# Long convolutions in one float32 pass, with the pointwise stage in place in PSUM and a skewed order on VectorE and ScalarE

## The chip, the cores and the metric

The kernel runs on one core of a Trainium2 chip. The metric is the device time of one execution in microseconds (us); 3 runs of the kernel before gave 2292.52, 2295.47 and 2297.69, so its median is 2295.47 us. All engines are named as the profile names them: PE is TensorE, PEld its weight loads, DVE VectorE, ACT ScalarE, POOL GpSimd, SP SyncE (here it only issues DMAs).

## The reference, cut to what matters

The model is a two-layer diffusion backbone of 512 latent and 256 context tokens with 1024 channels. Layer 0 mixes tokens with an order-2 Hyena long convolution, and then has a mixture of experts; layer 1 has attention and another mixture of experts. The change touches only the long convolutions of layer 0:

```python
def long_conv(z, K):
    L = z.shape[1]
    Z = jnp.fft.rfft(z.astype(jnp.float32), n=2 * L, axis=1)
    y = jnp.fft.irfft(Z * K[None], n=2 * L, axis=1)[:, :L]
    return y.astype(z.dtype)

def hyena_mix(h, w_in, b_in, conv_w, conv_b, ..., skip, w_out, b_out):
    u = short_conv(h @ w_in + b_in, conv_w, conv_b)
    v, x1, x2 = jnp.split(u, 3, axis=-1)
    K = hyena_filter_spectrum(L, ...)
    z = v
    for o, gate in enumerate((x1, x2)):
        z = gate * (long_conv(z, K[:, o]) + skip[o] * z)
    return z @ w_out + b_out
```

It runs once on the latent tokens (part x, 512 long) and once on the context tokens (part c, 256 long). The adaLN rows (`silu(c) @ ada_w + ada_b`) are a large product that has nothing to do with the convolution, and part of it is done beside it.

## The kernel before, in words

The transform is a product with tables of cosines and sines, split into even and odd frequencies. `hyena_conv` works through 8 units: 2 orders times 4 groups of 256 channels. A unit has three parts: x0, x1 (two halves of the latent frequencies) and c. In one unit's stretch of the program PE does, in this order: the forward products of part x0 (F0, tile ps_f), a turn of four 128x128 transposes that brings a third of the next unit's input into tile ps_z (T0), then F1, T1, F2, T2; then four products of the adaLN rows (`next(fill)`, L248), the inverse products of the unit before for its first 128 channels (I0, tile ps_y), adaLN products again, and I1. The first unit has no inverse beside it, and after the eighth there is a ninth stretch with inverses only. F0 to F2 here are names for PE's work; in the code F is the table of the transform.

Accuracy comes from splitting: a float32 value is held as a rounded high part and a low part (`split`, an ACT cast, L202, and a DVE subtraction, L203), and each product is three matmuls on fp32r operands (high by high, high by low, low by high; L726 forward, L769 inverse). The tables came in split form from the stage that computes the filter spectra (`k.F`), so they are in SBUF when the convolution starts. The context's inverse (L764) is already a plain float32 product.

Between forward and inverse product lies the pointwise stage of a part: ACT copies one half of ps_f to SBUF (L730), DVE forms sum and difference (L732, L733) into tile fab, the complex product with the spectrum kt is done by POOL (L737, L740) and DVE (L738, L739), DVE forms sum and difference once more (L741, L742), and the result is split into yh and yl (L748, L749). Each finished inverse is gated by DVE into U (L773). The spectra kt and the gates gx come from DRAM by SP's DMAs (L694, L699), each spectrum 512 KB, and the inputs hx were written there by POOL's DMAs (L665) in the stage before.

The order of PE is as the code is written (`tc.manual_schedule` for PE alone); those of DVE, ACT, POOL and SP are chosen by a scheduler, by its own estimates. On every engine the instructions run in the order that is fixed at build time, and one that waits holds up all behind it. PSUM has three buffers under tag a (ps_f, ps_y), one under tag b (ps_z) and one under tag m (ps_ada and ps_adaT): `Psum(k, a=3, b=1, m=1)`. The turn of the next unit (L709) thus needs ps_z to be read out by what reads it.

## Time and profile before

| what | value |
|---|---|
| median of 3 runs | 2295.47 us |
| profiled execution | 2298.74 us (3.27 above the median) |
| span in its trace, first to last instruction | 2296.9 us |
| mean granted TensorE clock over the span | 0.957 of full speed |
| PE, DVE, ACT, POOL busy | 89%, 56%, 33%, 21% of the span |
| convolution stage, first F0 to last inverse product | 376.3 to 590.1 us |

The shares are averages over stages with different limits. The convolution is 213.8 us, 9.3% of the span; what happens in it has to be read from windows of the trace over this stretch, and the end of it is followed by the output projection, which needs the last inverse. The eight F0 start at 376.3, 391.6, 422.7, 450.3, 474.7, 502.6, 525.7 and 551.6 us.

### The profile page before, as it was taken

The page shows a single profiled execution, that of the slowest core. Times are in us where ns is not written, and L with a number is a line of the kernel's source. Part 1 is how long each engine was busy: PE and PEld are TensorE (multiplying, and loading weights), DVE is VectorE, ACT ScalarE, POOL GpSimd, SP SyncE. Part 2 cuts the span into 40 slices and gives each one's busy share as a digit, 9 for nine tenths or more (in the row PEclk, how much of TensorE's full clock was granted, in tenths as well). Part 3 has the DMA queues.
Part 4 walks back from the last instruction along what each step waited for, and adds up shares of the span by engine and source line. Part 5 has one row for each costly group of instructions (what it writes and reads, how often), then busy time and mean ns, then how long its engine had stood idle before and what let it go on. Part 6 is the DMA issues. An engine that isn't in the chain of part 4 may idle for free.

```text
span 2296.9 us, 33948 instructions
## 1 busy us (share of the span) xinstructions
PE 2035.5 (89%) x13738; PEld 1196.9 (52%) x13738; DVE 1276.9 (56%) x2230; ACT 751.2 (33%) x1470; POOL 482.7 (21%) x472
## 2 busy tenths in 40 slices
PE   5899998788895999999999979999987698888797
PEld 2788887667672333333333269899756232222232
DVE  5877676999544344434344587787766133223233
ACT  4544443221332333222332245555533121111111
POOL 3333324666242000000000064243213000000000
PEclk9999999889896999999999979999998799999998
DMA  7434336545646999897997531111384999999996
GB/s 277 159 111 143 126 111 231 192 152 187 226 162 247 385 392 361 326 385 300 388 374 308 205 117 39 55 38 38 120 308 185 343 409 409 409 409 409 409 409 258
DMA packets 174342, 580.72 MB, mean 253 GB/s; under 512 B 11934, under 2 KB 42786, under 8 KB 167914
## 3 DMA queue, kind: packets, MB, share of 16 engines
q1 hardware_dynamic: 165226, 545.96, 62.4%
q0 software_dynamic: 8960, 32.59, 4.0%
q8 instruction: 108, 1.77, 0.3%
q14 instruction: 48, 0.39, 0.1%
HBM read 546.97 MB, written 31.54 MB: 252 GB/s over the span
## 4 chain that ended last, share of the span: by engine, by line
PE 49%; DMA 15%; DVE 12%; issue 3%; ACT 2%; POOL 1%; SPq 0%; DVEq 0%; POOLq 0%; ACTq 0%
PE ps_U L1225 10%; PE ps_Y L1225 9%; PE ps_G L1225 8%; PE ps_qkv L1653 6%; DMA raw<-in_moe_up_dram 5%; DMA raw<-in_moe_gate_dram 5%; PE ps_o L846 4%; DMA raw<-in_moe_down_dram 3%; PE ps_s L1401 3%; PE ps_sc L1721 1%; PE ps_pv L1752 1%; PE ps_H L1191 1%; DVE p L738 1%; DVE p L742 1%; DVE p L739 1%
## 5 line engine op out<-in xcount | busy, mean ns | idle before, releaser
L1225 PE MATMUL ps_Y<-raw,a 128*32 128x512 f32 (+1 forms) x1536 | 295.3, 600 | 28.5 <-DMA raw<-in_moe_down_dram 24.1
L1225 PE MATMUL ps_U<-raw,H 128*32 128x512 f32 (+1 forms) x1536 | 298.1, 597 | 17.0 <-DMA raw<-in_moe_up_dram 16.8
L1225 PE MATMUL ps_G<-raw,H 128*32 128x512 f32 (+1 forms) x1536 | 300.5, 606 | 12.8 <-DMA raw<-in_moe_gate_dram 11.7
L1225 PEld LDWEIGHTS ps_Y<-raw,a 128*32 128x32 f32 (+1 forms) x1536 | 78.4, 119 | 219.9 <-issue 171.3
L1180 POOL DMA_INDIRECT xe<-hscr,idxi x24 | 22.3, 927 | 728.4 <-PE ps_H L1191 655.2
L1225 PEld LDWEIGHTS ps_U<-raw,H 128*32 128x32 f32 (+1 forms) x1536 | 75.0, 118 | 186.2 <-issue 146.2
L1225 PEld LDWEIGHTS ps_G<-raw,H 128*32 128x32 f32 (+1 forms) x1536 | 76.6, 120 | 175.5 <-issue 153.1
L1653 PE MATMUL ps_qkv<-qwh,hh 128*128 128x256 f32 x512 | 154.0, 301 | 0.1
L1653 PE MATMUL ps_qkv<-qwl,hh 128*128 128x256 f32 x512 | 146.2, 285 | 3.8 <-POOL qwl L203 2.3
L1653 PE MATMUL ps_qkv<-qwh,hl 128*128 128x256 f32 x512 | 145.7, 285 | 0.0
L1268 DVE TENSOR_TENSOR up<-ps_U,lr 64x512 f32<-64x512 f32 (+1 forms) x48 | 41.2, 859 | 187.7 <-ACT lr L1265 182.6
L1268 DVE TENSOR_TENSOR sg<-ps_G,lr 64x512 f32<-64x512 f32 (+1 forms) x48 | 41.3, 859 | 162.9 <-ACT lr L1265 162.7
L1265 ACT COPY lr<-ps_Y 64x512 f32<-64x512 f32 (+1 forms) x47 | 33.8, 719 | 281.7 <-PE ps_Yc L1225 143.9
L1268 DVE TENSOR_TENSOR up<-ps_Y,lr 64x512 f32<-64x512 f32 (+1 forms) x47 | 40.0, 852 | 152.3 <-ACT lr L1265 152.3
L1225 PE MATMUL ps_Gc<-raw,H 128*32 128x512 f32 x512 | 121.4, 595 | 0.0
L1225 PE MATMUL ps_Uc<-raw,H 128*32 128x512 f32 x512 | 119.7, 596 | 0.0
L1225 PE MATMUL ps_Yc<-raw,a 128*32 128x512 f32 x512 | 116.6, 593 | 0.0
L1653 PEld LDWEIGHTS ps_qkv<-qwh,hh 128*128 128x128 f32 x512 | 98.9, 193 | 6.7 <-issue 4.9
L1653 PEld LDWEIGHTS ps_qkv<-qwl,hh 128*128 128x128 f32 x512 | 99.1, 194 | 4.6 <-POOL qwl L203 2.7
L642 PE MATMUL ps_u<-hh,wl 128*128 128x512 f32 (+1 forms) x384 | 101.3, 340 | 0.0
L642 PE MATMUL ps_u<-hh,wh 128*128 128x512 f32 (+1 forms) x384 | 100.9, 339 | 0.0
L642 PE MATMUL ps_u<-hl,wh 128*128 128x512 f32 (+1 forms) x384 | 100.7, 339 | 0.0
(475 smaller groups left out, 4786.9 us busy)
## 6 DMA issues: line engine op xcount, KB each, us to landing
raw<-in_moe_gate_dram SPq DMA_DIRECT2D x128, 1024.0 KB, 9.7
raw<-in_moe_up_dram SPq DMA_DIRECT2D x128, 1024.0 KB, 10.6
raw<-in_moe_down_dram SPq DMA_DIRECT2D x128, 1024.0 KB, 10.5
raw<-in_ada_w_dram SPq DMA_DIRECT2D x48, 1024.0 KB, 5.2
raw<-in_w_in_dram SPq DMA_DIRECT2D x12, 1024.0 KB, 5.4
raw<-in_w_qkv_dram SPq DMA_DIRECT2D x12, 1024.0 KB, 5.1
hx<-u POOLq DMA_DIRECT2D x24, 384.0 KB, 2.8
gx<-hx SPq DMA_DIRECT2D x16, 384.0 KB, 3.1
```

Of the source, the lines that this page charges most:

```text
L642: nc.tensor.matmul(ps[:, o:o + n], ww[:, d], ha[:, d, o:o + n], start=d == 0 and i == 0, stop=d == DC - 1 and i == 2)
L738: nc.vector.tensor_tensor(p1, ab, kv[:, :, 0:1].to_broadcast(shp), op=ALU.mult)
L739: nc.vector.tensor_tensor(p1[:, :, 0], p1[:, :, 0], p2[:, :, 1], op=ALU.subtract)
L742: nc.vector.tensor_tensor(p2[:, 1], p1[:, 0], p1[:, 1], op=ALU.subtract)
L846: nc.tensor.matmul(ps, a[d][:, tk], b, start=d == 0 and j == 0, stop=d == DC - 1 and j == 2 and bias is None)
L1191: nc.tensor.transpose(pt[:, d, :r], src[:r, c * P:(c + 1) * P], k.ident[:r, :r])
L1225: nc.tensor.matmul(ps[p0:p0 + n], st, w, start=start, stop=stop, tile_position=(0, p0))
L1265: nc.scalar.copy(t[:64], ps[64:])
L1268: nc.vector.tensor_tensor(out[:64, cs], ps[:64], t[:64], op=ALU.add)
L1401: nc.tensor.matmul(ps, o[:, c * P:(c + 1) * P], y[:, nb * 512:nb * 512 + 512], start=n == 0, stop=n == 2 * len(srcs) - 1)
L1653: nc.tensor.matmul(ps, a[:, d, tk], b, start=d == 0 and i == 0, stop=d == DC - 1 and i == 2)
L1721: nc.tensor.matmul(pss[m][:, o:o + n], a[r, tk], b[r, o:o + n], start=i == 0, stop=i == 2)
```

## The change

Nothing ahead of the convolution and nothing behind it changes its order on any engine. Within it:

- Forward and inverse products are one plain float32 matmul each in place of three fp32r matmuls; z and y are no longer split. The trace writes a plain float32 matmul as two records (L1775 and L764 of before are such).
- The tables Fx0, Fx1 (512 KB each), Fc0, Fc1 and idftx are loaded anew in float32 by SP's DMAs, in the pool of the convolution; the split ones stay where they are, unused. The SBUF range of Fx0 overlaps that of one of the input stage's tiles u, which is the source of the last write of hx (the DMA at L665), so its load waits for that write.
- The pointwise stage works in place in ps_f: sum and difference by DVE back into PSUM, one ACT copy of the whole tile (1024 columns) into fab, the second product by POOL from fab, the first by DVE in PSUM, the combination by DVE in PSUM, one ACT copy and a last DVE sum and difference into y. POOL has one instruction per part where it had three.
- From the first unit to the eighth the order of DVE and ACT is fixed as the code is written. Each part is cut into `begin`, `combine` and `end`, and the last two of a part stand inside the `begin` of the next part.

```diff
-    F, IE = k.F, {}
-    TILES = {"zh": ([P, 6, Q], F32R, 2, ca), "zl": ([P, 6, Q], F32R, 2, ca), "kt": ([P, 4, Q], F32, 4, ca),
-             "fab": ([P, 2, 2, Q], F32, 2, ca), "p1": ([P, 2, 2, Q], F32, 2, ca), "p2": ([P, 2, 2, Q], F32, 2, ca),
-             "yh": ([P, 2, 2, Q], F32R, 4, cb), "yl": ([P, 2, 2, Q], F32R, 4, cb), "p2c": ([P, 2, 2, Q], F32, 2, cb)}
+    F, IE = {}, {}
+    TILES = {"z": ([P, 6, Q], F32, 2, ca), "kt": ([P, 4, Q], F32, 4, ca),
+             "e": ([P, 2, Q], F32, 3, ca), "fab": ([P, 2, 2, Q], F32, 3, ca), "p2": ([P, 2, 2, Q], F32, 3, ca),
+             "y": ([P, 2, 2, Q], F32, 4, cb), "yc": ([P, 2, 2, Q], F32, 2, cb)}
...
-            Z[q, o] = tile_of("zh"), tile_of("zl")
-        zh, zl = Z[q, o]
+            Z[q, o] = tile_of("z")
...
-        pv = pt.rearrange("p c j t -> p c (j t)")
-        split(k, zh[:, 2 * c2:2 * c2 + 2], zl[:, 2 * c2:2 * c2 + 2], pv)
+        nc.scalar.copy(Z[q, o][:, 2 * c2:2 * c2 + 2], pt.rearrange("p c j t -> p c (j t)"))
...
-        for par, (Fh, Fl) in enumerate(F[pt]):
+        for par in range(2):
             for s in range(2):
-                n = 0
                 for h in range(nh):
...
-                    for w, m in ((fh, a), (fh, b), (fl, a)):
-                        nc.tensor.matmul(pk[:, par, s], w, m, start=n == 0, stop=n == 3 * nh - 1)
-                        n += 1
-        p2 = tile_of("p2" if pt == "x" else "p2c")
+                    nc.tensor.matmul(pk[:, par, s], F[pt][par][:, h, s, fs], z[:, c0 + par * nh + h],
+                                     start=h == 0, stop=h == nh - 1)
+        y = Y[q, o, pt, j] = tile_of("y" if pt == "x" else "yc")
+        return pk, y, kt.rearrange("p (a s) q -> p a s q", a=2), [tile_of(n) for n in ("e", "fab", "p2")]
+
+    def begin(f, prev):
+        pk, y, kv, (e, ab, p2) = f
+        shp = [P, 2, 2, Q]
         nc.scalar.copy(e, pk[:, 0])
...
+        if prev:
+            combine(prev)
+        nc.vector.tensor_tensor(pk[:, 0], e, pk[:, 1], op=ALU.add)
+        nc.vector.tensor_tensor(pk[:, 1], e, pk[:, 1], op=ALU.subtract)
+        nc.scalar.copy(ab, pk)
+        if prev:
+            end(prev)
         nc.gpsimd.tensor_tensor(p2, ab, kv[:, :, 1:2].to_broadcast(shp), op=ALU.mult)
-        nc.vector.tensor_tensor(p1, ab, kv[:, :, 0:1].to_broadcast(shp), op=ALU.mult)
-        nc.vector.tensor_tensor(p1[:, :, 0], p1[:, :, 0], p2[:, :, 1], op=ALU.subtract)
...
+        nc.vector.tensor_tensor(pk, pk, kv[:, :, 0:1].to_broadcast(shp), op=ALU.mult)
+
+    def combine(f):
+        pk, y, kv, (e, ab, p2) = f
+        nc.vector.tensor_tensor(pk[:, :, 0], pk[:, :, 0], p2[:, :, 1], op=ALU.subtract)
+        nc.vector.tensor_tensor(pk[:, :, 1], pk[:, :, 1], p2[:, :, 0], op=ALU.add)
+        nc.scalar.copy(e, pk[:, 0])
+
+    def end(f):
+        pk, y, kv, (e, ab, p2) = f
+        nc.vector.tensor_tensor(y[:, 0], e, pk[:, 1], op=ALU.add)
+        nc.vector.tensor_tensor(y[:, 1], e, pk[:, 1], op=ALU.subtract)
...
-                        for w, m in ((a, ih), (a, il), (b, ih)):
-                            nc.tensor.matmul(out, w, m, start=n == 0, stop=n == 6 * nf - 1)
...
+                for n in range(2 * nf):
+                    f, s = n // 2, n % 2
+                    t = IE[pt][:, par, f, s] if pt == "c" else F["x"][1][:, f, s] if par else IE["x"][:, f, s]
+                    nc.tensor.matmul(out, Y[q, o, pt, f][:, par, s, js], t, start=n == 0, stop=n == 2 * nf - 1)
...
+    for pt, L, nf in (("x", LX, 2), ("c", LC, 1)):
+        n = nf * L
+        F[pt] = [cb.tile([P, nf, 2, L // 2], F32, name="F%s%d" % (pt, par)) for par in range(2)]
+        for par, t in enumerate(F[pt]):
+            nc.sync.dma_start(t.rearrange("p a b c -> p (a b c)"), k.A["dft" + pt][:, par * n:par * n + n])
     load(*units[0])
     load(*units[1])
-    IE["x"], = load_dft(k, [cb], "idftx", (2, 2, LX // 2))
+    IE["x"] = cb.tile([P, 2, 2, LX // 2], F32, name="idftx")
+    nc.sync.dma_start(IE["x"].rearrange("p a b c -> p (a b c)"), k.A["idftx"])
...
+    order = tc.manual_schedule(engines=ORDERED)
+    order.__enter__()
     for i in range(len(units) + 1):
...
+        f = None
         if i < len(units):
             load_gates(*units[i])
+        else:
+            order.__exit__(None, None, None)
         for c2 in range(3):
             if i < len(units):
-                forward(*units[i], *parts[c2])
+                g = forward(*units[i], *parts[c2])
+                begin(g, f)
+                f = g
...
@@ -802,6 +810,9 @@
             next(fill, None)
             if i:
                 inverse(*units[i - 1], j)
+            if f and j == 0:
+                combine(f)
+                end(f)
```

Three places show how the instructions stand. First ACT's row for one unit in the middle, before; p2 is the copy of ps_f, zh the cast of a turn, yh the cast of the result:

```order
L730 COPY p2_4273<-ps_f_4248 128x512
L202 CAST zh_4291<-ps_z_4293 128x512
L730 COPY p2_4325<-ps_f_4300 128x512
L202 CAST zh_4291<-ps_z_4343 128x512
L730 COPY p2c_4363<-ps_f_4350 128x512
L202 CAST zh_4291<-ps_z_4375 128x512
L748 CAST yh_4285<-p2_4273 128x512 x2
L748 CAST yh_4337<-p2_4325 128x512 x2
```

The casts of the turns stand directly behind the copies of the forward products. Now the same for the change, where e is the copy of ps_f (L730, and L746 a second one after the combination), fab the copy of the whole tile and z that of a turn:

```order
L730 COPY e_4134<-ps_f_4124 128x512
L735 COPY fab_4135<-ps_f_4124 128x1024
L709 COPY z_4143<-ps_z_4144 128x512
L730 COPY e_4160<-ps_f_4150 128x512
L746 COPY e_4134<-ps_f_4124 128x512
L735 COPY fab_4161<-ps_f_4150 128x1024
L709 COPY z_4143<-ps_z_4174 128x512
L730 COPY e_4186<-ps_f_4180 128x512
L746 COPY e_4160<-ps_f_4150 128x512
```

The copy of turn T1, the second z here, stands behind the second fab, which reads what DVE's sum and difference of part x1 wrote.

On DVE, the change's row around those: L733 and L734 are sum and difference, L739 the product, L743 and L744 the combination with POOL's product p2, L750 and L751 the end:

```order
L733 TENSOR_TENSOR ps_f_4124<-e_4134,ps_f_4124 128x512
L734 TENSOR_TENSOR ps_f_4124<-e_4134,ps_f_4124 128x512
L739 TENSOR_TENSOR ps_f_4124<-ps_f_4124,kt_3975 128x1024
L743 TENSOR_TENSOR ps_f_4124<-ps_f_4124,p2_4136 128x2x256
L744 TENSOR_TENSOR ps_f_4124<-ps_f_4124,p2_4136 128x2x256
L733 TENSOR_TENSOR ps_f_4150<-e_4160,ps_f_4150 128x512
L734 TENSOR_TENSOR ps_f_4150<-e_4160,ps_f_4150 128x512
L750 TENSOR_TENSOR y_4133<-e_4134,ps_f_4124 128x512
L751 TENSOR_TENSOR y_4133<-e_4134,ps_f_4124 128x512
L739 TENSOR_TENSOR ps_f_4150<-ps_f_4150,kt_3977 128x1024
```

The sum and difference of the second part (tile ps_f_4150) stand behind the combination of the first (ps_f_4124), and this reads p2, which POOL computes from the first fab.

The second place is SP's queue at the start of the stage, from the third input on, before:

```order
L690 DMA U2_3801<-hx2_795 128x768
L694 DMA kt_3820<-kscr_00x0_401 128x1024
L694 DMA kt_3822<-kscr_00x1_436 128x1024
L694 DMA kt_3824<-kscr_00c0_523 128x1024
L690 DMA U3_3802<-hx3_796 128x768
L694 DMA kt_3828<-kscr_01x0_1121 128x1024
L781 DMA iec_3840<-in_idftc_dram 128x256
L782 DMA iec_3840<-in_dftc_dram 128x256
L699 DMA gx_3866<-hx8_801 128x768
L699 DMA gx_3866<-hx9_802 128x768
```

and now:

```order
L690 DMA U2_3801<-hx2_795 128x768
L775 DMA Fx0_3818<-in_dftx_dram 128x1024
L775 DMA Fx1_3819<-in_dftx_dram 128x1024
L775 DMA Fc0_3822<-in_dftc_dram 128x256
L775 DMA Fc1_3823<-in_dftc_dram 128x256
L694 DMA kt_3828<-kscr_00x0_401 128x1024
L694 DMA kt_3830<-kscr_00x1_436 128x1024
L694 DMA kt_3832<-kscr_00c0_523 128x1024
L690 DMA U3_3802<-hx3_796 128x768
L694 DMA kt_3836<-kscr_01x0_1121 128x1024
L779 DMA idftx_3842<-in_idftx_dram 128x1024
L782 DMA iec_3844<-in_idftc_dram 128x256
L783 DMA iec_3844<-in_dftc_dram 128x256
L699 DMA gx_3868<-hx8_801 128x768
```

The four tables F (L775) have moved ahead of all spectra kt, and idftx ahead of iec.

The third place is the end of the first group of adaLN rows, on DVE: L251 adds the bias to what PE summed in ps_ada, and PE's transposes of its result (L261) come right behind turn T2 in the stretch of the fifth unit. Before:

```order
L741 TENSOR_TENSOR p2_4542<-p1_4547 128x512
L742 TENSOR_TENSOR p2_4542<-p1_4547 128x512
L251 TENSOR_TENSOR adarow_4003<-ps_ada_4005,adarow_4003 128x512
L739 TENSOR_TENSOR p1_4585<-p1_4585,p2c_4580 128x2x256
L749 TENSOR_TENSOR yl_4555<-p2_4542,yh_4554 128x512
L773 SCALAR_TENSOR_TENSOR U5_3804<-ps_y_4642,invx_221,gx_4245 128x512
L773 SCALAR_TENSOR_TENSOR U5_3804<-ps_y_4642,invc_222,gx_4245 128x256
L741 TENSOR_TENSOR p2c_4580<-p1_4585 128x512
L742 TENSOR_TENSOR p2c_4580<-p1_4585 128x512
L732 TENSOR_TENSOR fab_4709<-p2_4707,ps_f_4682 128x512
L733 TENSOR_TENSOR fab_4709<-p2_4707,ps_f_4682 128x512
```

and now:

```order
L733 TENSOR_TENSOR ps_f_4456<-e_4462,ps_f_4456 128x512
L734 TENSOR_TENSOR ps_f_4456<-e_4462,ps_f_4456 128x512
L750 TENSOR_TENSOR y_4435<-e_4436,ps_f_4426 128x512
L751 TENSOR_TENSOR y_4435<-e_4436,ps_f_4426 128x512
L739 TENSOR_TENSOR ps_f_4456<-ps_f_4456,kt_4257 128x1024
L251 TENSOR_TENSOR adarow_3953<-ps_ada_3955,adarow_3953 128x512
L266 COPY modT_625<-ps_adaT_4488 128x4x2 x4
L768 SCALAR_TENSOR_TENSOR U6_3805<-ps_y_4497,invx_221,gx_4259 128x512
L768 SCALAR_TENSOR_TENSOR U6_3805<-ps_y_4497,invc_222,gx_4259 128x256
```

The addition stood ahead of the sums and differences of the unit whose turns precede the transposes (L732 and L733 of a new ps_f); now it stands behind the product of that unit's third part.

## Rows read from the trace of the kernel before

**Rows 1.** Busy time in stretches; columns stand in the first line.
```profile
core 0: us, PE busy (x) PEld busy (x) DVE busy (x) ACT busy (x) POOL busy (x), PEclk, DMA share, GB/s
422.70:450.30 27.60, 22.34 (x156) 18.89 (x154) 27.60 (x29) 5.78 (x10) 15.85 (x10) 0.81 0.47 169
...
551.64:590.10 38.46, 29.85 (x220) 26.19 (x219) 35.55 (x46) 14.85 (x24) 27.51 (x17) 0.87 0.40 138
376.30:590.10 213.80, 169.29 (x1213) 145.21 (x1214) 208.37 (x235) 55.36 (x94) 136.25 (x78) 0.88 0.54 191
```

**Rows 2.** DVE's costliest groups, 370 to 600 us: busy us, mean ns | idle before.
```profile
L738 DVE TENSOR_TENSOR p<-fab,kt 128x1024 f32<-128x1024 f32 x24 | 48.1, 2004 | 0.0
...
L773 DVE SCALAR_TENSOR_TENSOR U<-ps_y,invx,gx 128x512 f32<-128x512 f32 x16 | 11.9, 741 | 1.8 <-PE ps_y L764 1.8
...
L732 DVE TENSOR_TENSOR fab<-p,ps_f 128x512 f32<-128x512 f32 x16 | 10.8, 676 | 2.5 <-ACT p L730 2.5
...
L742 DVE TENSOR_TENSOR p2c<-p 128x512 f32<-128x512 f32 x8 | 5.4, 678 | 0.0
```

**Rows 3.** Timeline of DVE: start us, us, instruction.
```profile
431.38 0.68 DVE L732 TENSOR_TENSOR fab<-p,ps_f 128x512 f32<-128x512 f32 x1
431.97 0.68 DVE L733 TENSOR_TENSOR fab<-p,ps_f 128x512 f32<-128x512 f32 x1
```

**Rows 4.** Waits, 376 to 590 us: total us, times, longest.
```profile
PE ps_z L709 <- DVE zl L203: 31.7, 13, 4.3
```

**Rows 5.** Timeline of PE at the start: start us, us, instruction.
```profile
376.32 0.38 PE L726 MATMUL ps_f<-zh,dftx0h 128*128 128x256 f32 x1 [0.34 <-ACT zh L202]
```

**Rows 6.** Timeline of POOL, same place.
```profile
378.66 0.55 POOL L665 DMA_DIRECT2D hx<-u  x1 [0.62 <-issue]
```

**Rows 7.** Timeline of ACT, same place.
```profile
381.83 0.59 ACT L730 COPY p<-ps_f 128x512 f32<-128x512 f32 x1 [4.58 <-PE ps_f L726]
```

**Rows 8.** Timeline of SP's queue, same place.
```profile
385.60 0.91 SPq L699 DMA_DIRECT2D gx<-hx  x2
```

**Rows 9.** Waits of SP's queue, 350 to 420 us.
```profile
SPq L699 <- DMA hx<-u: 9.8, 1, 9.8
```

**Rows 10.** Tile hx, 340 to 420 us: time from issue to landing.
```profile
DMA to landing us min/median/max: 2.6/6.2/9.4
```

**Rows 11.** DMA issues, 350 to 420 us: KB each, median us to landing.
```profile
kt<-kscr_02c SPq DMA_DIRECT2D x1, 512.0 KB, 4.5
```

**Rows 12.** ACT's groups, 370 to 600 us.
```profile
L730 ACT COPY p<-ps_f 128x512 f32<-128x512 f32 x16 | 9.4, 586 | 22.8 <-PE ps_f L726 17.9 <-DVE yl L749 2.7 <-issue 2.2
...
L202 ACT CAST idftx0h<-raw 128x1024 fp32r<-128x1024 f32 x1 | 1.1, 1050 | 0.0
```

**Rows 13.** The products on POOL: min/median/max ns.
```profile
L737 POOL TENSOR_TENSOR p<-fab,kt x16: 2349/2372/3377, 383.9 to 563.3; 128x1024 f32<-128x1024 f32 x16
```

**Rows 14.** Timeline of PE, 256 columns in attention (L1653 fp32r, L1775 plain float32).
```profile
1471.90 0.28 PE L1653 MATMUL ps_qkv<-qwh,hl 128*128 128x256 f32 x1
1472.02 0.59 PE L1775 MATMUL ps_rb<-osq,ones 128*128 128x256 f32 x2
1472.45 0.49 PE L1742 MATMUL ps_aTt<-ident,p 128*128 128x128 f32 x3
```

**Rows 15.** Timeline of PE, float32 matmuls of 128 columns.
```profile
589.07 1.05 PE L764 MATMUL ps_y<-iec,p2c 128*128 128x128 f32 x8
```

**Rows 16.** Timeline of PE after two of the waits of rows 4.
```profile
433.31 1.12 PE L709 MATMUL ps_z<-ident,U 128*128 128x128 f32 x4 [4.17 <-DVE zl L203]
```

**Rows 17.** The same, the other wait.
```profile
462.92 1.11 PE L709 MATMUL ps_z<-ident,U 128*128 128x128 f32 x4 [2.70 <-DVE zl L203]
463.96 1.94 PE L248 MATMUL ps_ada<-raw,cs 128*32 128x512 f32 x8
```

**Rows 18.** Stretches after these two waits, columns as in rows 1.
```profile
432.00:442.00 10.00, 7.60 (x32) 5.31 (x33) 10.00 (x10) 1.76 (x3) 6.16 (x4) 0.50 0.20 73
462.60:466.20 3.60, 3.28 (x14) 1.29 (x15) 3.60 (x3) 0.59 (x1) 2.19 (x1) 0.53 0.27 107
```

More of the change, by code (lines that the diff above doesn't have):

```diff
@@ L709, in turn @@
                 nc.tensor.transpose(pt[:, c, j], U[2 * q + j][:, cc * P:(cc + 1) * P], k.ident)
-        pv = pt.rearrange("p c j t -> p c (j t)")
-        split(k, zh[:, 2 * c2:2 * c2 + 2], zl[:, 2 * c2:2 * c2 + 2], pv)
+        nc.scalar.copy(Z[q, o][:, 2 * c2:2 * c2 + 2], pt.rearrange("p c j t -> p c (j t)"))
     def forward(q, o, pt, c0, nch, nf, j):
-        zh, zl = Z[q, o]
+        z = Z[q, o]
         nh = nch // 2
@@ L728, in forward @@
-        p2 = tile_of("p2" if pt == "x" else "p2c")
-        e = p2[:, 0]
-        nc.scalar.copy(e, pk[:, 0])
-        ab = tile_of("fab")
-        nc.vector.tensor_tensor(ab[:, 0], e, pk[:, 1], op=ALU.add)
-        nc.vector.tensor_tensor(ab[:, 1], e, pk[:, 1], op=ALU.subtract)
-        kv = kt.rearrange("p (a s) q -> p a s q", a=2)
-        p1 = tile_of("p1")
-        shp = [P, 2, 2, Q]
-        nc.gpsimd.tensor_tensor(p2, ab, kv[:, :, 1:2].to_broadcast(shp), op=ALU.mult)
-        nc.vector.tensor_tensor(p1, ab, kv[:, :, 0:1].to_broadcast(shp), op=ALU.mult)
@@ L739, in forward @@
-        nc.vector.tensor_tensor(p1[:, :, 0], p1[:, :, 0], p2[:, :, 1], op=ALU.subtract)
-        nc.gpsimd.tensor_tensor(p1[:, :, 1], p1[:, :, 1], p2[:, :, 0], op=ALU.add)
-        nc.vector.tensor_tensor(p2[:, 0], p1[:, 0], p1[:, 1], op=ALU.add)
-        nc.vector.tensor_tensor(p2[:, 1], p1[:, 0], p1[:, 1], op=ALU.subtract)
-        if pt == "c":
-            Y[q, o, pt, j] = p2
-            return
-        yh, yl = Y[q, o, pt, j] = tile_of("yh"), tile_of("yl")
-        for i, eng in enumerate((nc.vector, nc.gpsimd)):
-            nc.scalar.copy(yh[:, i], p2[:, i])
-            eng.tensor_tensor(yl[:, i], p2[:, i], yh[:, i].bitcast(F32), op=ALU.subtract)
+                    nc.tensor.matmul(pk[:, par, s], F[pt][par][:, h, s, fs], z[:, c0 + par * nh + h],
+                                     start=h == 0, stop=h == nh - 1)
@@ L759, in inverse @@
                 out = py[:, base + par * L // 2:base + (par + 1) * L // 2]
-                n = 0
-                for f in range(nf):
-                    for s in range(2):
-                        if pt == "c":
-                            nc.tensor.matmul(out, Y[q, o, pt, f][:, par, s, js], IE[pt][:, par, f, s], start=s == 0, stop=s == 1)
-                            continue
-                        a, b = (y[:, par, s, js] for y in Y[q, o, pt, f])
-                        ih, il = (t[:, f, s] for t in (F[pt][1] if par else IE[pt]))
-                        for w, m in ((a, ih), (a, il), (b, ih)):
-                            nc.tensor.matmul(out, w, m, start=n == 0, stop=n == 6 * nf - 1)
-                            n += 1
+                for n in range(2 * nf):
+                    f, s = n // 2, n % 2
+                    t = IE[pt][:, par, f, s] if pt == "c" else F["x"][1][:, f, s] if par else IE["x"][:, f, s]
+                    nc.tensor.matmul(out, Y[q, o, pt, f][:, par, s, js], t, start=n == 0, stop=n == 2 * nf - 1)
         ch = 2 * q + j
```

2 lines of the change are left out of this document (removed).

## Prediction

> **What bounds the kernel now.** I read the stretches from one F0 to the next first, since the shares of the whole span say nothing of a stage that is 9% of it. In the convolution DVE is busy 208.4 of 213.8 us while PE is busy 169.3, at a mean granted clock of 0.88 [rows 1]. DVE has hardly a gap in any unit, so it is the bound, and PE's waits say how it is felt: 13 times a turn waits until DVE has made zl from the turn before, 31.7 us in all [rows 4]. The groups by form show why DVE is so slow: the product L738 takes 2.00 us on average over 1024 columns of operands in SBUF [rows 2], and POOL's product beside it 2.37 [rows 13]. After the waits PE runs at the lower of its two clock levels for a while: behind one of 4.17 us the granted clock is 0.50 from 432 to 442, behind one of 2.70 us it is 0.53 for 3.6 us [rows 16 to 18]. Five units from 422.70 to 551.64 take 128.9 us, 25.8 each; the last F0 to the last inverse takes 38.5 [rows 1].
>
> **Prices.** PE, at full clock: a plain float32 matmul of 256 columns stands as two records and the next instruction starts 0.43 later [rows 14]; one of 128 columns takes a quarter of 1.05 us [rows 15] less the drain, 0.23. Then F0 and F1 are 8 x 0.43 = 3.44 each, F2 1.72, one inverse 8 x 0.43 + 4 x 0.23 = 4.34. A turn of four transposes takes 1.04 to the next start at the low level and four adaLN products 1.94 [rows 17], so I take half, 0.5 and 0.95. A unit of PE work: 3.44 + 3.44 + 1.72 + 3 x 0.5 + 2 x 0.95 + 2 x 4.34 = 20.7, against the 25.8 of now.
>
> DVE: 512 columns with an operand in PSUM take 0.68 (L732) [rows 2]. DVE results written into PSUM are shown nowhere in this trace; the bounds are half and double of 0.68 (the nearest rows are L732 with one PSUM operand and L742 with none, equal at 0.68, so I take 0.68; double adds 6 x 0.68 = 4.1 us to the chain below). The product of 1024 columns in place I take at 1.21, twice 0.60. DVE's sum for a unit is 3 x (6 x 0.6 + 1.2) = 14.4, 0.6 between starts of such steps [rows 3], and the two gatings U 2 x (0.74 [rows 2] + half as much) = 2.2, about 17: the bound of before is gone. What is late next is a chain.
>
> ACT: 0.59 for 512 columns from PSUM, and 1.05 for 1024 (measured from SBUF) [rows 12]. POOL: 2.37 [rows 13].
>
> **The new wait.** ps_z has one buffer, so turn T2 may start only when ACT has copied T1. In ACT's fixed row that copy stands behind the second part's fab, this behind DVE's sum and difference of the second part, these behind the first part's combination, and this behind POOL's product of the first part, which needs the first fab. PE executes in order: behind T2 are queued the adaLN products, both inverses and the next F0, so all of PE stands. From the end of F0: copy 0.59, sum and difference 1.36, fab 1.05, POOL 2.37, combination 1.36, sum and difference 1.36, fab 1.05, copy of T1 0.59: 9.7, with handovers 9.9. PE's own work in that time is T0, F1, T1, F2 = 6.2. So PE waits 3.7 us in each unit.
>
> **The sum, on the profiled execution (2298.74).**
> A, the start. Before, F0 starts at 376.32 [rows 5] with the tables in place, and ends when its copy starts, 381.83 [rows 7]. Now the load of Fx0 waits on SP for the last write of hx, issued at 378.66 [rows 6]. An hx transfer lands 2.6 to 9.4 us after issue, median 6.2 [rows 10]; before, SP's first gx waited for that same write (9.8 us [rows 9]) and went at 385.60 [rows 8], which is the upper bound. I choose the fastest, 381.3, since only one transfer is waited for. The table is 512 KB like a kt, 4.5 us [rows 11]: F0 starts at 385.8, lasts some 5 us (3.44 at the high clock, 6.9 at the low), and ends at 390.8: +9 (+6 to +15). The spectra queued behind the tables on SP come later too, but are used only after F0.
> B, the first two units. The first has no inverse beside it: 9.9 + 0.5 + 1.9 + 3.44 = 15.7 from F0's end to the next, against 12.7 (391.6 plus 2.9 of matmuls, less 381.83): +3.0. In the second, forward products follow each other without inverses between and wait for the three buffers of tag a: 24.4 (below) and the 5 us of one part on DVE, 29.5, against 31.1: −1.6. Together +1.4.
> C, five units: 9.9 + 0.5 + 0.95 + 4.34 + 0.95 + 4.34 + 3.44 = 24.4 against 25.8: −7.
> D, the end of the first adaLN group. PE's transposes behind T2 in the fifth unit wait for DVE's addition L251, which now stands behind that unit's third product: after the second fab come POOL 2.37, combination 1.36, sum and difference 1.36, end 1.36, product 1.21 and the addition 0.68, less the 1.04 of T1's copy and T2 that pass meanwhile: +7 once (before, the addition was done a unit earlier).
> E, the tail. From the last F0 on: F0 3.44, then three parts in the chain, 6.7 + 6.1 + 6.1, the last end 2, and two inverses 8.7: 33.1 against 38.46 [rows 1]: −5.4. Its price rests on the same chain.
> F, the clock. The above has PE at full speed, but each of seven units now holds a wait of 3.7 us, between the two shown above [rows 16, 17]. Behind the shorter one 3.6 us at 0.53 cost 1.7 us, behind the longer one 7.6 busy us at 0.50 cost 3.8 [rows 18]. All of PE's work behind T2 is on the path. I take 1.7 x 7 = +12 (0 to +27), since POOL and DVE are not on the path right behind it.
> Sum: 9 + 1.4 − 7 + 7 − 5.4 + 12 = +17. Behind the convolution everything waits for its last inverse, so the end moves one for one. 2298.74 + 17 = 2315.7 for a profiled execution; this one stands 3.27 above the median of three, so against that median 2312.
>
> What I cost at nothing: the split of z and y goes away on ACT, DVE and POOL; ACT is busy 5.8 of some 26 us per unit [rows 1] and has room for 3 x 1.05 more. The tables loaded anew are 1.8 MB (three of 512 KB, two of 128) on a queue that has gaps; only the first is on the path, in A.
>
> **The rivals.**
> R1, faster: DVE writes PSUM in half the time. The chain's six DVE steps shrink by 0.34 each, to 7.9; PE waits 1.7 us instead of 3.7 and stays at the high clock. F falls away (−12), seven units win 2 (−14), the tail 3: 2283. For it: with F gone the sum is +5, so it is faster from 0.7 us less of wait per unit (5 / 7), a wait of 3 us; against it: L732 and L742 cost the same whatever they read, so the memory hardly sets the pace.
> R2, no change: the waits are too short to lower the clock, and DVE's steps follow 0.60 apart instead of 0.68. F goes (−12), the chain is 0.5 shorter (−3.5): +1.5, 2297. Against it: 2.70 us of waiting was followed by 0.53.
> R3, much slower: each wait costs what the one at 433 did, 3.8 x 7 = 27, and the table is let go only at 385.60, 4 us later: 2312 + 15 + 4 = 2331. For it: 3.7 us is nearer to 4.17 than to 2.70.
> R4, slower by price: a plain float32 matmul takes four spacings of an fp32r matmul. These are 0.12 [rows 14], so 0.48 for 0.43; 24 such matmuls behind T2 and in the next F0 per unit at 0.05 give 1.2, eight units 9 to 10: 2321. The Trainium skill says this in "FP8 and Floating Point Precision", section TensorE Precision Notes: true float32 makes four passes through the array. This trace disagrees by a tenth, since the next instruction started 0.43 later and only two records stand there; by that row nothing is added.
>
> **Chances and range.** About 0.2% (4.6 us) can be told from no change here: 2290.9 to 2300.1. The forecast (slower, between 2301 and 2326) 0.54, R1 0.15, R2 0.14, R3 0.14, R4 0.03. Faster 0.15, same 0.14, slower 0.71. The forecast's own range, 2301 to 2326, comes from A's −3 to +6 and F's −8 to +8. To hold 8 in 10 it takes in R2 down to 2291 and part of R3: 2291 to 2327.
>
> **What will show it.** F0's first matmul at about 386 with a wait on a DMA of Fx0, not at 376; PE's wait before each T2 for ACT's copy of z, 3.7 us, seven times, with the granted clock near 0.5 behind it; DVE's writes to PSUM at 0.68; DVE busy about 17 of 24 us in a unit, POOL 3 x 2.37; one wait of 7 us before the transposes L261; stretches from F0 to F0 of 24.4 plus what the clock takes. Wrong would be a first F0 below 380, waits at T2 under 2 us, or DVE steps other than 0.6 to 0.7; a convolution that ends before 590 by the trace would refute the sum as a whole.

## The result and the profile after

Measured beside the kernel before, the changed kernel takes 2320.18 us (median of 4 runs, 2316.41 to 2322.39) against 2296.58 (4 runs, 2292.52 to 2297.84): 1.0095 times as long, 95% interval 1.0077 to 1.0113, which is 18 to 26 us more. The forecast was 2312 in a range of 2291 to 2327. The profiled execution is the fastest of the four, 2316.41 us with a span of 2314.6.

First the stretches from one F0 to the next (of the third to the sixth unit; the seventh takes 27.56), then the tail from the last F0 and the whole convolution; they answer to [rows 1]:

```profile
core 0: us, PE busy (x) PEld busy (x) DVE busy (x) ACT busy (x) POOL busy (x), PEclk, DMA share, GB/s
434.16:461.74 27.58, 23.64 (x118) 17.99 (x117) 17.60 (x25) 7.92 (x12) 7.07 (x3) 0.88 0.46 166
461.74:488.62 26.88, 22.93 (x118) 17.93 (x117) 17.60 (x25) 7.93 (x12) 7.09 (x3) 0.94 0.44 164
488.62:522.45 33.83, 23.31 (x114) 19.01 (x113) 18.58 (x30) 7.92 (x12) 9.07 (x7) 0.80 0.34 114
522.45:550.26 27.81, 23.86 (x118) 18.14 (x117) 17.61 (x25) 7.92 (x12) 7.07 (x3) 0.88 0.45 152
...
577.82:612.42 34.60, 30.27 (x167) 24.47 (x166) 26.84 (x44) 15.84 (x24) 13.16 (x9) 1.00 0.47 158
384.82:612.42 227.60, 186.59 (x925) 144.40 (x926) 147.56 (x218) 71.11 (x108) 64.70 (x34) 0.90 0.50 179
```

DVE was busy throughout a stretch before; now it has 18 us of work in some 27.5, and PE 23.6. No engine is full: what is left is a chain that goes through several. The convolution ends at 612.42 in place of 590.12, 22.3 us later. The tail is shorter (34.60 for 38.46), the stretches are longer (27.5 for 25.8), and one of them takes 33.83.

The waits in the convolution (total, times, longest), the answer to [rows 4]:

```profile
PE ps_z L708 <- ACT z L709: 28.4, 8, 4.2
...
PE ps_f L721 <- DMA Fx<-in_dftx_dram: 9.8, 1, 9.8
...
PE ps_adaT L261 <- DVE adarow L251: 6.6, 1, 6.6
```

These are the three places that the prediction named: turns that wait for ACT's copy, the start that waits for the table, and the transposes of the adaLN rows. A steady stretch shows the first of them step by step, here over all engines (columns as in the timelines above):

```profile
437.62 0.60 PE L708 MATMUL ps_z<-ident,U 128*128 128x128 f32 x4
437.81 0.59 ACT L730 COPY e<-ps_f 128x512 f32<-128x512 f32 x1 [5.83 <-PE ps_f L721]
...
438.43 0.70 DVE L733 TENSOR_TENSOR ps_f<-e,ps_f 128x512 f32<-128x512 f32 x1 [2.93 <-ACT e L730]
439.17 0.69 DVE L734 TENSOR_TENSOR ps_f<-e,ps_f 128x512 f32<-128x512 f32 x1
439.95 1.01 ACT L735 COPY fab<-ps_f 128x1024 f32<-128x1024 f32 x1 [1.55 <-DVE ps_f L734]
...
441.04 2.36 POOL L738 TENSOR_TENSOR p<-fab,kt 128x1024 f32<-128x1024 f32 x1 [11.85 <-ACT fab L735]
...
442.00 1.89 PE L721 MATMUL ps_f<-z,Fc 128*128 128x256 f32 x8
...
443.43 0.70 DVE L743 TENSOR_TENSOR ps_f<-ps_f,p 128x512 f32<-128x512 f32 x1 [1.20 <-POOL p L738]
444.16 0.70 DVE L744 TENSOR_TENSOR ps_f<-ps_f,p 128x512 f32<-128x512 f32 x1
444.77 0.69 DVE L733 TENSOR_TENSOR ps_f<-e,ps_f 128x512 f32<-128x512 f32 x1
...
445.49 0.69 DVE L734 TENSOR_TENSOR ps_f<-e,ps_f 128x512 f32<-128x512 f32 x1
...
446.27 1.01 ACT L735 COPY fab<-ps_f 128x1024 f32<-128x1024 f32 x1 [0.74 <-DVE ps_f L734]
...
447.18 0.59 ACT L709 COPY z<-ps_z 128x512 f32<-128x512 f32 x1
...
447.83 1.11 PE L708 MATMUL ps_z<-ident,U 128*128 128x128 f32 x4 [3.94 <-ACT z L709]
...
448.87 1.94 PE L248 MATMUL ps_ada<-raw,cs 128*32 128x512 f32 x8
```

Read it by the starts: copy e at 437.81, sum and difference, fab at 439.95, POOL's product at 441.04, the combination at 443.43, the next part's sum and difference at 444.77, its fab at 446.27, and only then the copy of turn T1 at 447.18, for which turn T2 stood since 443.9. PE's last work before, the products of part c, began at 442.00. Behind the wait the four transposes take 1.11 us instead of 0.60, and the adaLN products 1.94.

The start, in place of [rows 5], [rows 7] and [rows 8]; the three timelines are those of PE, ACT and SP's queue:

```profile
384.82 1.62 PE L721 MATMUL ps_f<-z,Fx 128*128 128x256 f32 x3 [9.83 <-DMA Fx<-in_dftx_dram]
```
```profile
390.11 0.59 ACT L730 COPY e<-ps_f 128x512 f32<-128x512 f32 x1 [14.45 <-PE ps_f L721]
```
```profile
380.61 0.81 SPq L775 DMA_DIRECT2D Fx<-in_dftx_dram  x2
```

DVE's groups from 370 to 620 us, in place of [rows 2, 3], and POOL's:

```profile
L739 DVE TENSOR_TENSOR ps_f<-ps_f,kt 128x1024 f32<-128x1024 f32 x24 | 29.6, 1232 | 9.0 <-ACT fab L735 9.0
...
L743 DVE TENSOR_TENSOR ps_f<-ps_f,p 128x512 f32<-128x512 f32 x24 | 16.7, 697 | 20.6 <-POOL p L738 20.6
...
L733 DVE TENSOR_TENSOR ps_f<-e,ps_f 128x512 f32<-128x512 f32 x24 | 16.5, 689 | 31.2 <-ACT e L730 31.2
...
L750 DVE TENSOR_TENSOR y<-e,ps_f 128x512 f32<-128x512 f32 x16 | 10.9, 678 | 0.0
```
```profile
L738 POOL TENSOR_TENSOR p<-fab,kt 128x1024 f32<-128x1024 f32 x24 | 56.6, 2359 | 162.9 <-ACT fab L735 162.9
```

A result written to PSUM costs DVE 0.69 to 0.70 against 0.68 to SBUF, and the product of 1024 columns takes 1.23 with POOL at work beside it, where L738 of before took 2.00.

The clock behind the wait, and later in the same stretch, answering to [rows 18]:

```profile
447.80:453.60 5.80, 5.77 (x21) 3.32 (x22) 4.53 (x7) 2.05 (x4) 1.92 (x1) 0.57 0.33 121
456.30:461.70 5.40, 5.40 (x33) 4.15 (x33) 3.73 (x6) 0.59 (x1) 0.00 (x0) 1.00 0.84 296
```

It is granted 0.57 for 5.8 us behind the wait of 3.94, and the full clock after that. The price is not the same each time: in the stretch from 461.74 the turn behind a wait of 3.95 still took 0.66 us, the clock fell later and for less long, and the stretch is 26.88 us instead of 27.6 to 27.8.

### The profile page after: what moved, and what is told of

It reads as the page before. It is cut to its first block, busy times and chain, and to the rows that moved or that the text cites. A ratio compares the mean times of both kernels' runs of the same rounds, so it can differ in the third digit from the quotient of the medians.

```text
span 2314.6 us, 33323 instructions
## 1 busy us (share of the span) xinstructions
PE 2051.7 (89%) x13450; PEld 1198.2 (52%) x13450; DVE 1219.0 (53%) x2214; ACT 767.0 (33%) x1485; POOL 417.5 (18%) x431
## 4 chain that ended last, share of the span: by engine, by line
PE 61%; DMA 15%; DVE 9%; issue 8%; POOL 3%; ACT 3%; SPq 0%; DVEq 0%; POOLq 0%; ACTq 0%
PE ps_U L1236 9%; PE ps_Y L1236 9%; PE ps_u L642 9%; PE ps_G L1236 8%; PE ps_qkv L1664 7%; DMA raw<-in_moe_gate_dram 6%; PE ps_o L857 4%; DMA raw<-in_moe_up_dram 4%; DMA raw<-in_moe_down_dram 3%; PE ps_s L1412 3%; POOL p L738 2%; PE ps_k L459 2%; PE ps_sc L1732 1%; PE ps_pv L1763 1%; PE ps_H L1202 1%
## 5 line engine op out<-in xcount | busy, mean ns | idle before, releaser
L1191 POOL DMA_INDIRECT xe<-hscr,idxi x24 | 22.3, 929 | 728.1 <-PE ps_H L1202 687.8
L1276 ACT COPY lr<-ps_Y 64x512 f32<-64x512 f32 (+1 forms) x47 | 33.8, 719 | 282.0 <-PE ps_Yc L1236 143.9
```

Of the source, the lines that this page charges most:

```text
L1276: nc.scalar.copy(t[:64], ps[64:])
```

## The experiments

The theory: the start that waits for the write of hx, the chain through ACT's fab ahead of each turn with the low clock behind it, and the late addition L251 are three separate prices, and the single pass itself gains. The rivals: the plain float32 products and their clock set the length and the waits only show it; or the order fixed on DVE and ACT is at fault as a whole. Ratios are to the kernel before on the same chip, with 95% intervals; five rounds each. Against them stands 1.0095 for the changed kernel. The kernel before had medians of 2298.9 to 2300.0 us on these chips, against 2296.58 above, so the differences to the changed kernel and to other runs are taken from the ratios.

**e1, turns copied first.** ACT's copy of a turn goes ahead of fab.

```diff
         nc.scalar.copy(e, pk[:, 0])
+        if mid:
+            turn(*mid)
         if prev:
             combine(prev)
...
-                begin(g, f)
+                begin(g, f, nxt and (*nxt[0], c2))
                 f = g
-            if nxt:
-                turn(*nxt[0], c2)
```

> The changed kernel with ACT's copy of each turn placed directly behind the copy e of the same part, ahead of fab, so that turn T2 no longer stands behind the second fab; PE's and DVE's order as they are. Theory (the wait at T2 and the low clock behind it make the steady units long): the 3.94 us waits at T2 go below 1 us; what is late next is the chain of the three parts itself (0.59 + 3 x 6.1 + 2 to the release of ps_f for the next F0, about 21 us, plus F0 3.4), so stretches from F0 to F0 fall from 27.6 to 24.5, seven of them 20 us less: about 2300. Rival (the plain float32 products on PE and their clock set the length, the wait only shows it): stretches stay within 1 us of 27.6, 2317 to 2320.

Measured 2308.58 us, 1.0037 (1.0026 to 1.0049): some 13 us less than the changed kernel. The stretches are 24.1 to 25.0 as expected, but the wait of the fifth grew. PE's waits in one stretch, and ahead of the transposes in the next:

```profile
475.35 1.97 PE L767 MATMUL ps_y<-idftx,y 128*128 128x256 f32 x8 [2.26 <-DVE y L753]
...
481.69 1.96 PE L767 MATMUL ps_y<-idftx,y 128*128 128x256 f32 x8 [0.76 <-DVE y L753]
...
507.46 1.12 PE L261 MATMUL ps_adaT<-ident,adarow 128*128 128x128 f32 x4 [11.25 <-DVE adarow L251]
```

No turn waits in a steady stretch any more. The inverse products wait in their place, for a buffer of ps_f that DVE's end L753 has to release: the chain of the parts is next, 24 us long. The transposes L261 wait 11.25 us instead of 6.58, since PE reaches them sooner. The expectation had 3 us less in each of seven units, 20 in all. The four steady stretches gave that; the fifth is as long as before (33.96 for 33.83), and so are the first two units together (49.9 for 49.3).

**e2, tables clear of the hx write.** idftx becomes the first tile of its pool.

```diff
+    IE["x"] = cb.tile([P, 2, 2, LX // 2], F32, name="idftx")
     for pt, L, nf in (("x", LX, 2), ("c", LC, 1)):
...
     load(*units[1])
-    IE["x"] = cb.tile([P, 2, 2, LX // 2], F32, name="idftx")
     nc.sync.dma_start(IE["x"].rearrange("p a b c -> p (a b c)"), k.A["idftx"])
```

> The changed kernel with idftx as the first tile of its pool, so that the tables F lie 4 KB higher and their loads wait for no write of hx; nothing else. Theory (the start is late because the table waits for that write): the first F0 starts at 377 to 379 in place of 384.8, the end of the convolution comes 6 to 8 us earlier, 2312 to 2314. Rival (the start is hidden by later waits, for spectra or buffers): F0 starts early but the third F0 comes when it did, 2318 to 2321.

Measured 2310.28 us, 1.0048 (1.0033 to 1.0062): 11 us less. The first F0 waits for nothing:

```profile
374.43 3.62 PE L721 MATMUL ps_f<-z,Fx 128*128 128x256 f32 x16
```

It starts 10.4 us sooner and runs at the high clock from the start, and the convolution ends at 600.66, 11.8 sooner. Nothing later hides the start. The expected 6 to 8 were too few because F0 starts 3 us ahead of the expected 377, and because without the wait it also takes 3.62 us instead of 5.25.

**e3, the addition of the adaLN rows early.**

```diff
+        if kc == DC - 1 and l == 0:
+            nc.vector.tensor_tensor(row, ps, row, op=ALU.add)
         yield kc
-    nc.vector.tensor_tensor(row, ps, row, op=ALU.add)
+    if l:
+        nc.vector.tensor_tensor(row, ps, row, op=ALU.add)
```

> The changed kernel with the bias addition of an adaLN group (L251) placed on DVE right behind the group's last products, as the kernel before had it in effect. Theory: the 6.58 us wait of the transposes L261 goes, with the low clock behind it about 7 us in all: 2313. Rival (the chain of the parts holds the fifth stretch as long in any case): the stretch falls from 33.8 by less than 3 us, 2317 or more.

Measured 2314.37 us, 1.0064 (1.0048 to 1.0081): 7 us less, with the fifth stretch at 27.02 instead of 33.83. As the theory had it.

**e4, the order of DVE and ACT left to the scheduler.** The two calls that fix it are taken out (`order.__enter__()`, `order.__exit__(...)`).

> The changed kernel without the fixed order on DVE and ACT: the scheduler chooses it, PE's order stays as written. It puts the copies of the turns directly behind the copies e, and fab behind them. Theory (the fixed order, not the in-place stage or the single pass, costs the time): the waits at T2 go below 1.5 us, the stretches fall to 24 to 25.5, 2295 to 2305 with the late start still in it. Rival (the in-place stage has a longer chain than the old one whatever the order): 2315 or more.

Measured 2306.5 us, 1.0032 (1.0016 to 1.0048). The time is near the theory's upper end, but only in part for its reason: no T2 waits in a steady stretch any more, but the stretches stay at 26.3 to 27.4. The waits have only moved, as PE's row of one stretch shows:

```profile
470.82 3.75 PE L765 MATMUL ps_y<-idftx,y 128*128 128x256 f32 x8 [3.53 <-DVE y L751]
```

The turns pass, and the first inverse waits 3.53 us for the end of the first part, with the low clock behind it. The gain lies elsewhere: the first two units take 44.3 us to the third F0 instead of 49.3, and the fifth stretch has no wait for L251 and takes 27.4 instead of 33.8. So in a steady unit the fixed order costs next to nothing against the scheduler's (27.5 and 27.0 on average); the in-place chain is there in either.

**e5, sum and difference straight to SBUF.**

```diff
-        nc.vector.tensor_tensor(pk[:, 0], e, pk[:, 1], op=ALU.add)
-        nc.vector.tensor_tensor(pk[:, 1], e, pk[:, 1], op=ALU.subtract)
-        nc.scalar.copy(ab, pk)
+        nc.vector.tensor_tensor(ab[:, 0], e, pk[:, 1], op=ALU.add)
+        nc.vector.tensor_tensor(ab[:, 1], e, pk[:, 1], op=ALU.subtract)
...
-        nc.vector.tensor_tensor(pk, pk, kv[:, :, 0:1].to_broadcast(shp), op=ALU.mult)
+        nc.vector.tensor_tensor(pk, ab, kv[:, :, 0:1].to_broadcast(shp), op=ALU.mult)
```

> The changed kernel with the first sum and difference written by DVE straight into fab in SBUF, the product from there into ps_f; ACT's copy fab of 1024 columns is gone, the rest of the order as it is. Theory (the chain from F0 to the release of T2 and of ps_f sets the length): two fab copies of 1.0 leave the chain to T2 and ACT's copy of T1 no longer stands behind one, the wait falls from 3.94 to 0.7; the stretches fall from 27.6 to 22, 2283 to 2290. Rival (the place that counts is PSUM: with both operands in SBUF DVE and POOL hold each other up again, as L738 of before at 2.0 us on average): the product takes 2 to 3 us in place of 1.23, the stretches stay above 25, 2303 or more.

Measured 2303.85 us, 1.0024 (1.0014 to 1.0034): 16 us less, the rival's number. The wait at T2 fell to 2.03 and the four steady stretches to between 23.75 and 24.9, so the fab copies did count; the fifth grew to 35.4, with a wait of 9.82 us for L251. But DVE and POOL hold each other up:

```profile
L738 DVE TENSOR_TENSOR ps_f<-fab,kt 128x1024 f32<-128x1024 f32 x24 | 49.3, 2052 | 0.3
```
```profile
L737 POOL TENSOR_TENSOR p<-fab,kt 128x1024 f32<-128x1024 f32 x24 | 64.4, 2684 | 138.2 <-DVE fab L734 130.3 <-issue 7.9
```

2.05 us for the product instead of 1.23, and 2.68 instead of 2.36 on POOL, only because the first operand lies in SBUF; the result goes to PSUM as before. The timeline shows how:

```profile
436.29 1.23 DVE L738 TENSOR_TENSOR ps_f<-fab,kt 128x1024 f32<-128x1024 f32 x1
436.39 3.34 POOL L737 TENSOR_TENSOR p<-fab,kt 128x1024 f32<-128x1024 f32 x1 [9.94 <-DVE fab L734]
...
442.51 2.37 POOL L737 TENSOR_TENSOR p<-fab,kt 128x1024 f32<-128x1024 f32 x1 [2.79 <-DVE fab L734]
...
443.49 2.48 DVE L738 TENSOR_TENSOR ps_f<-fab,kt 128x1024 f32<-128x1024 f32 x1
```

Where DVE begins first, it takes its 1.23 us and POOL ends 2.2 us after it; where POOL begins first, it takes 2.37 and DVE ends 1.1 us after it. They do not share, one stands until the other is done. Both theories are half right here.

**e6 to e8, together.** e6 is e1, e2 and e3 in one; e7 adds the edit of e5; e8 adds halves to e6:

```diff
         nc.vector.tensor_tensor(pk[:, 0], e, pk[:, 1], op=ALU.add)
+        nc.scalar.copy(ab[:, 0], pk[:, 0])
         nc.vector.tensor_tensor(pk[:, 1], e, pk[:, 1], op=ALU.subtract)
-        nc.scalar.copy(ab, pk)
+        nc.scalar.copy(ab[:, 1], pk[:, 1])
...
-        nc.gpsimd.tensor_tensor(p2, ab, kv[:, :, 1:2].to_broadcast(shp), op=ALU.mult)
+        for a in range(2):
+            nc.gpsimd.tensor_tensor(p2[:, a], ab[:, a], kv[:, a, 1:2].to_broadcast(shp[:1] + shp[2:]), op=ALU.mult)
```

> The three single changes together: turns copied first, tables clear of the hx write, early addition of the adaLN rows. Theory (the three are separate places on the path): in e1 the wait before the transposes was 11.25 us, so the gains add to 13 + 11 + 11: 2285, faster than before. Rival (they overlap, what one gives back another takes): 2295 or more.

> e6 with the sum and difference straight to SBUF as in e5. Theory: 24.1 per stretch in e1 is the chain of three parts; 1.0 less in each part leaves 21 to 22, near PE's own 20.7: 15 to 18 us below e6, about 2269. Rival (DVE and POOL hold each other up): no gain over e6 or a loss.

> e6 with ACT's fab copy and POOL's product cut in two halves each, so that POOL starts on the sum while DVE makes the difference. Theory: per part 0.68 + 0.59 + 2 x 1.3 in place of 1.36 + 1.05 + 2.37, 0.9 less; stretches of 21.5 to 22, 12 to 15 us below e6, about 2272. Rival (the parts are not the bound once turns are early, PE and its clock are): within 4 us of e6.

e6: 2293.64 us, 0.9973 (0.9962 to 0.9984). The three gains were 0.58, 0.47 and 0.31% one by one, 1.36 together; e6 is 1.22 below the changed kernel, the same within the intervals. So they are separate prices, though my 2285, 0.9950 of the kernel before, was 5 us too low (the fifth stretch is still 28.2, with a wait of 3.17 us ahead of the adaLN products that follow the transposes). e7: 2289.0, 0.9959 (0.9945 to 0.9972), some 3 us below e6 with intervals that overlap, where 15 to 18 were expected: DVE's product takes 2.05 us again, and the stretches are 24.7 for 25.0. Most of the gain of e5 is eaten by the hold-up, nearly the rival's case. e8: 2283.19, 0.9934 (0.9916 to 0.9952), 9 us below e6: less than the 12 to 15 expected, as the stretches are still 24.8 or 23.4 and the first inverse waits 2.03 us for a buffer. The wait is the same in the longer ones and in the shorter; behind it the inverse products take 2.6 to 3.6 us, at the low clock, in the longer ones and 1.97 in the shorter.

**e9 and e12, adaLN products into that wait.** e9 is e8 with both pairs of adaLN products ahead of the first inverse, e12 the same except in the fifth stretch:

```diff
+        split_fill = i in (4, len(units))
+        for _ in range(0 if split_fill else 2):
+            next(fill, None)
         for j in range(2):
-            next(fill, None)
+            if split_fill:
+                next(fill, None)
```

> e8 with both pairs of adaLN products ahead of the first inverse (one used to stand between the two inverses). In e8 the first inverse waits 2.03 us in each steady unit until DVE's end of the first part frees its ps_f buffer. Theory (that wait and the low clock behind it are what keeps the stretches at 24.8 instead of 20.7): 0.95 us of work moves into it, the wait falls to about 1.1 and the clock dips less, stretches 23 to 24, 5 to 12 us below e8. Rival (the second inverse then waits for its buffer as much longer): within 3 us of e8.

> e9 with the old places in the fifth stretch alone (the transposes L261 ahead of the first inverse, the one pair of adaLN products that follows them between the inverses). In e9 the steady stretches fell from 24.8 to 23.4, and the fifth had a wait of 9.84 us before the second pair. Theory (two changes of the same kernel that cancelled): the fifth stretch falls from 31.8 to about 25.8 and the rest stays, 6 us below e9 and below e8: about 2279. Rival (what the convolution wins is lost behind it): within 3 us of e8 and e9.

e9: 2287.63 us, 0.9947 (0.9931 to 0.9963), no better than e8, though the steady stretches fell to 23.4: the fifth takes 31.8 and had this,

```profile
485.17 1.94 PE L248 MATMUL ps_ada<-raw,cs 128*32 128x512 f32 x8 [9.84 <-issue]
```

a wait of 9.84 us: the trace has DVE's copies out of ps_adaT at 484.69, just ahead of it, and ps_ada and ps_adaT share the one buffer of tag m. The profile names no releaser, so that it is this buffer is inferred; with the old places in e12 the wait is 1.20. e12: 2281.6 us, 0.9926 (0.9913 to 0.9940), the lowest ratio of this study, 17 us below the kernel before. Its steady stretches are 23.4 with the waits cut into pieces of 1.2 and 1.3 us, and the clock stays up, by the row of one of them:

```profile
420.40:443.83 23.43, 20.97 (x118) 17.16 (x117) 17.35 (x26) 8.41 (x15) 7.64 (x6) 1.00 0.53 191
```

The fifth takes 25.84, as expected, and by the traces e12's convolution is 6.9 us shorter than e8's (199.1 and 206.0). In the time e12 is only 2 us below e8, within the intervals, which is the rival's number: the program behind took 1703.0 us in the one trace and 1698.5 in the other. So the 6 us are shown for the stage and not for the kernel.

**e10, the single pass alone.** The matmuls, tables and copies of the change, with the pointwise stage in SBUF as it was (tile p1, POOL's second instruction) and the order chosen by the scheduler.

```diff
+        nc.vector.tensor_tensor(p1, ab, kv[:, :, 0:1].to_broadcast(shp), op=ALU.mult)
+        nc.vector.tensor_tensor(p1[:, :, 0], p1[:, :, 0], p2[:, :, 1], op=ALU.subtract)
+        nc.gpsimd.tensor_tensor(p1[:, :, 1], p1[:, :, 1], p2[:, :, 0], op=ALU.add)
+        nc.vector.tensor_tensor(y[:, 0], p1[:, 0], p1[:, 1], op=ALU.add)
+        nc.vector.tensor_tensor(y[:, 1], p1[:, 0], p1[:, 1], op=ALU.subtract)
```

> One part of the change alone: single float32 products and unsplit z and y, but the pointwise stage in SBUF with the kernel before's instructions on DVE and POOL, and the order of DVE and ACT chosen by the scheduler; tables loaded late as in the changed kernel. Theory (the in-place stage and the fixed order cost, the single pass gains): DVE loses 3 x 0.6 of zl and 2 x 0.6 of yl per unit, stretches of 23 in place of 25.8, less 20, plus 9 for the start: 2286 to 2292. Rival (DVE and POOL holding each other up in SBUF is what bounds, so the single pass alone gains nothing): 2300 or more.

Measured 2289.05 us, 0.9952 (0.9937 to 0.9967): 11 us faster than the kernel before, with the late start still in it, and 33 faster than the changed kernel. Two of its stretches:

```profile
451.45:472.54 21.09, 21.09 (x118) 17.07 (x117) 18.70 (x23) 3.22 (x6) 12.58 (x6) 1.00 0.59 211
472.54:501.79 29.25, 22.76 (x115) 18.33 (x113) 26.96 (x33) 3.22 (x6) 17.80 (x12) 0.88 0.51 179
```

Three of the five take 21.0 to 21.1, and PE is busy all the time in them, near its own 20.7, although DVE's product takes 1.76 on average over the stage. The other two take 26.3, with a wait of 3.25 us for DVE's gating L755, and 29.3 in the fifth, with one of 4.96 us ahead of the adaLN products. Against e4, which also leaves the order to the scheduler, e10 differs in the pointwise stage alone: 1.0032 against 0.9952, so the stage in place costs 18 us. The changed kernel against e4 gives 14 us for the fixed order. This is the division of the change: the single pass gains 11 us with the late start in it, the stage in place costs 18 and its order 14.

**e11, the wait filled with work.** The products of part c are issued three times, which adds 3.4 us of PE work per unit.

```diff
-        for par in range(2):
-            for s in range(2):
+        for par, s in [(p, s) for _ in range(3 if pt == "c" else 1) for p in range(2) for s in range(2)]:
```

> The changed kernel with the forward products of part c issued three times over (the same result each time), so that 3.4 us of PE work stand in the wait ahead of T2, which stays where it is. Theory (the clock falls because PE stood still, and that costs 2 to 2.8 us per unit behind T2): the waits at T2 shrink to 0.5, the products behind it run at the high level, stretches fall from 27.6 to about 25, seven times: 2302 to 2308, faster by more work. Rival (the low clock has another reason, or the added work delays the parts): 2318 or more.

Measured 2317.25 us, 1.0070 (1.0055 to 1.0085): 6 us less than the changed kernel with more work, though not the 12 to 18 expected. PE's row of the turn after the filled wait, and the stretches:

```profile
449.93 0.66 PE L708 MATMUL ps_z<-ident,U 128*128 128x128 f32 x4 [0.49 <-ACT z L709]
450.51 1.07 PE L248 MATMUL ps_ada<-raw,cs 128*32 128x512 f32 x8
```
```profile
461.49:486.73 25.24, 24.76 (x135) 19.94 (x134) 17.61 (x26) 7.92 (x12) 7.08 (x3) 1.00 0.50 176
449.90:455.70 5.80, 5.78 (x34) 4.36 (x35) 4.52 (x7) 2.04 (x4) 1.93 (x1) 1.00 0.52 173
```

Turn T2 comes 10.2 us after the end of F0 in both kernels, but the clock is 1.00 behind it where it was 0.57, and the stretch is 25.24 in place of 27.46 on average. So 2.2 us of a steady unit are the clock's. The gain holds in four stretches. The first two units became 1.6 us longer to the third F0, of which 1.3 lie in the first F0, whose products ran at the low clock for longer (6.53 us for 5.25), ahead of any added work; and the fifth is 34.6, because the transposes still wait.

## Why the prediction was right, step by step

The forecast had the sign, the three places and the mechanism of each; the size was 5 us short in the convolution: +17, against +22.3 by the trace. In terms of F0's starts:

- **A and B** (forecast 9 + 1.4, and the clock of two units, 3.4: 13.8). The third F0 starts at 434.16 instead of 422.70, +11.5. The table's load was let go at 380.61 (forecast 381.3), F0 started at 384.82 (385.8) and its copy at 390.11 (390.8). e2 shows that this place is worth 11 us. Most of the 2.3 too many are the clock of the first unit: its T2 waited only 2.11 us, and F0 of the second unit behind it took 3.72, so the full clock was kept.
- **C and F**, the unit. Forecast 24.4 and 1.7 for the clock, 26.1; the four steady stretches average 27.46. The wait at T2 is 3.94 (forecast 3.7). The term that was mis-sized most is F, the clock: it was taken from the wait of 2.70 us [rows 17, 18], and e11 shows 2.2 in place of 1.7, between that row's price and the 3.8 behind the longer wait. The other 0.8 is C itself, 25.24 with the clock up. By e11's rows 0.3 of it lie ahead of T2, which starts 10.2 us after the end of F0 for the forecast 9.9 (DVE's steps of 0.69 to 0.70 for 0.68, and handovers), and 0.5 behind it, where PE needs 11.56 us to the next F0 for the forecast 11.08.
- **D** was +7 and is 33.83 − 27.46 = 6.4, a wait of 6.58; e3 gives 7 us back.
- **E** was −5.4 and is 34.60 − 38.46 = −3.9, 1.5 more: the last two inverses start 0.9 later than forecast, at 603.03, and take 9.4 us for 8.7, with the transposes L261 between them.

The sum by the trace is 11.5 + 14.7 (third to eighth F0, 143.66 against 128.94) − 3.9 = 22.3. The terms missed both ways: A and B by 2.3 too much, the units by 6.2 too little, the tail by 1.5. Between profiled executions the total moved less, 17.7, and between medians 23.6; the program behind the convolution took 1702.2 us in the trace after and 1706.8 in the one before, which no step of the change explains, and which lies within the spread of runs (1698.5 to 1711.4 in the traces of all kernels here). So it is luck that the profiled execution, 2316.41, lies 0.7 from the forecast 2315.7; the convolution itself was 5 us longer than forecast.

The rivals: R1 needed DVE to write PSUM at half the price, and the rows say 0.69. R2 needed the clock to stay up, and it was 0.57. R3 needed the load to wait until 385.60 and 3.8 us of clock per unit; it was let go at 380.61, and e11 puts the clock at 2.2. R4, the price of a plain float32 product, did not come, since sixteen records of F0 start at 434.16 and the turn follows at 437.62, 0.43 each for eight products. But its sentence on the Trainium skill was read wrongly by me: 0.43 us at 2.4 GHz is four cycles for each of the 256 columns, that is four passes of one cycle per column. Four passes are what "FP8 and Floating Point Precision" of the Trainium skill, section TensorE Precision Notes, says of true float32. The trace agrees with the rule. The 0.12 between fp32r products is a little longer than the 0.107 of one such pass, and that made the price of R4 too high.

What I did not see: the prediction blamed the place of T1's copy in ACT's order, and e1 and e4 show that with the copy moved the chain waits at the next buffer, so that the stretches still take 24 to 25 us in e1 and 26.3 to 27.4 in e4. The deeper reason is that three parts pass one after another through ACT, DVE, POOL and DVE, and that ps_f is not free before the end of each; the single pass without the in-place stage (e10) shows no such wait in three of its five stretches. That e10 with the edits of e2 and e3 would be faster than e12 is likely, but was not run.
